# The opening of a hybrid retention and attention layer: first loads on two queues, rows scaled in two parts, products in another order

## The chip, the cores and the metric

The kernel runs on one core of a Trainium2 chip. The metric is the device time of one execution in microseconds, lower is better. Before the change the median of three runs is 1394.26 us (1393.91 to 1397.99).

A core has a matrix engine (TensorE, PE in the profile, with its weight loads shown as PEld), a vector engine (VectorE, DVE), a scalar engine (ScalarE, ACT), a general engine (GpSimd, POOL) and an engine that only issues transfers (SyncE, SP). SP and ACT can both issue transfers; each has a queue of its own, served by the same 16 DMA engines.

## The reference, cut to what matters

```python
h_lat = rms_norm(x, norm1_g) * (1.0 + sc1) + sh1        # x: 1024 x 1024, sc1 and sh1 from silu(c) @ w_mod
h_ctx = rms_norm(ctx, norm1_g) * (1.0 + csc1) + csh1    # ctx: 256 x 1024
p = h_lat @ w_in                                        # 1024 x 3584, split into heads:
# 4 heads of bidirectional chunkwise retention, 4 heads of differential attention
x = x + g1 * (concat(retention, attention) @ w_out)
h2 = rms_norm(x, norm2_g) * (1.0 + sc2) + sh2
x = x + g2 * conv_ffn(h2)                               # gated MLP with a depthwise convolution
return rms_norm(x, final_g)
```

All of it is in 32-bit floats. The change touches the first two lines and the first block of `w_in` (512 columns, the attention's values); the rest of the kernel stands as it was.

## The kernel before, in words

A product of two 32-bit matrices is made of three matrix products of rounded parts: each operand is split into a high part (rounded) and a low part (the rest), and `high x high`, `high x low` and `low x high` are summed in PSUM. `passes` issues these three (L131 to L133). ACT makes the high parts, DVE or POOL the low parts by a subtraction.

The opening works on the first 512 rows of `x` as four tiles of 128 rows (`xs0`; the order lists call them xs_171 to xs_174, here rows 0 to 3) and on the next 512 as `xs1`. The names are these:

- `cl` holds small vectors, `csil` is silu of the conditioning, spread into `cz`; `ident` is the identity that transposes use; `fold` is made of it.
- `mod_load(d, q)` loads half q of the modulation weights for the d-th 128 columns into a tile `wt`; `mod_part` multiplies them with `cz` into `pr` (L513); `mod_row` copies the result to `rw` (ACT); `mod_sums` turns it with `fold` into `pm` and makes the scale and shift `mcol` (DVE, L524 and L525).
- `square` (ACT, into `sq`) and `power` (DVE, then POOL) give a row's factor in `sm`; `scale` multiplies the row by it (DVE, L535).
- `modulate` transposes the d-th 128 columns of the rows into `pt` (PE, L541), applies `mcol` and writes the high part of `hT` (ACT, L544), the same in full into `tmp` (DVE, L546) and the low part of `hT` (L548), on POOL for odd d and on DVE for even d. `latents` calls it for `xs0` and `xs1`, `context` for the context rows. There are three `pt` banks and two `tmp` buffers.
- `w_load` loads `w_in` into `raw`, `w_split` splits it into `whi` (ACT, L569) and `wlo` (DVE, L571). A `raw` tile holds two of the eight steps k; the first is loaded and split in halves.
- `part_products(ts, k)` adds step k to the output tiles `ts`, two at a time. `turn_over` issues products of ones whose result is thrown away, while PE has nothing else.

The loop over k interleaves all this: products of tiles 0 and 1, some preparation, products of tiles 2 and 3, more preparation for later steps. From k = 6 on the second half of the rows is transposed and modulated, for two further output tiles. `in_order(begin)` at its end keeps every engine of PE, DVE, ACT and SP in the order in which the code was written. What is written first therefore goes first on its engine, and a queue waits for its head.

Of the kernel before, what the change touches and what calls it, by code (L numbers as in the profile page):

```python
# [17 lines left out]
P = 128  # L18
D = 1024
KD = D // P  # L20
# [52 lines left out]
def kernel(  # L73
# [80 lines left out]
    with ExitStack() as p1:  # L154
# [343 lines left out]
        with ExitStack() as p0:  # L498
# [38 lines left out]
            def modulate(tiles, d, who, hi, lo):  # L537
# [9 lines left out]
                eng = nc.gpsimd if d % 2 else nc.vector  # L547
# [10 lines left out]
            def w_load(kk, i0=0, i1=2):  # L558
                if i0 == 0:
                    raws.append(wr.tile([P, 2, 512], F32, name="raw"))  # L560
                nc.sync.dma_start(out=raws[-1][:, i0:i1], in_=w_in[6][:, 2 * kk + i0 : 2 * kk + i1, :])
# [20 lines left out]
            def part_products(ts, k):  # L582
                if k > 0:
                    for t in ts:
                        passes(part[t], lat_lhs(t, k), wget(k, 0, 512), False, k == KD - 1)
                    return
                hi, lo = wget(k, 0, 512)
                for t in ts:
                    mm(part[t], lat_lhs(t, k)[0], hi, start=True, stop=False)
                for t in ts:  # L590
                    mm(part[t], lat_lhs(t, k)[0], lo, start=False, stop=False)
                if 3 in ts:
                    latents(0, 1)
                for t in ts:
                    mm(part[t], lat_lhs(t, k)[1], hi, start=False, stop=False)
# [8 lines left out]
            for t in range(2):  # L604
                load_row(t, nc.scalar)
            mod_load(0, 1)
            nc.sync.dma_start(out=ident, in_=consts[:, K_ID : K_ID + P])
            w_load(0, 0, 1)
            for t in range(2, 4):
                load_row(t)  # L610
            for q in range(2):
                mod_load(1, q)
# [8 lines left out]
            turn_over(2)  # L621
# [20 lines left out]
            square(xs0[3], 5)  # L642
            power(5)
            for q in range(2):
                mod_load(3, q)
            for k in range(KD):
                part_products((0, 1), k)
                if k == 0:
# [3 lines left out]
                    scale(xs0[2], 4, 0, 2 * P)  # L652
                    scale(xs0[3], 5, 0, 2 * P)
# [24 lines left out]
                if k == 0:  # L678
                    for t in range(1, 4):
                        scale(xs0[t], 2 + t, 2 * P, D)  # L680
# [22 lines left out]
                if k in (0, 2, 4):  # L703
                    w_split()
# [926 lines left out]
```

## Time and profile before

| | us |
|---|---|
| median of three runs | 1394.26 (1393.91 to 1397.99) |
| the profiled execution | 1398.66 |
| its span | 1396.9 |
| PE busy | 1365.7 (98%) |
| DVE busy | 1003.0 (72%) |
| ACT busy | 729.6 (52%) |
| POOL busy | 296.9 (21%) |

The profile shows one execution. A row of the order in time gives start and length in us, the engine, the source line, the operation, the output and input tiles, their sizes and the count; the bracket at its end is how long the engine had been idle before it and whose completion ended that. A row may hold several instructions that follow each other. A row of a window gives the window, its length, then the busy time of PE, PEld, DVE, ACT and POOL with the number of instructions, PE's granted clock (1.00 is full), the busy share of the DMA engines and GB/s.

### The profile page before, as it was taken

To read this page: it belongs to the slowest core of one execution; us is meant where nothing else is said; L and a number is where in the kernel's file an instruction comes from. 1 tells how busy PE (TensorE), PEld (TensorE's weight loads), DVE (VectorE), ACT (ScalarE), POOL (GpSimd) and SP (SyncE) were. 2 spreads that over 40 slices of the span, in tenths; PEclk is the share of its full clock that TensorE was granted. 3 is DMA by queue.
4 is the path that set the end of the run, shared out by engine and by line. 5 is a ranking of instruction groups with operands and counts; after the bars stand their busy time and mean duration, and the time that the engine had idled before them with its cause. 6 is when DMAs were issued, how large, how long until landed. Compare 5 with 4: busy or idle time off the path is not lost.

```text
span 1396.9 us, 19447 instructions
## 1 busy us (share of the span) xinstructions
PE 1365.7 (98%) x7038; PEld 1146.9 (82%) x7038; DVE 1003.0 (72%) x1462; ACT 729.6 (52%) x1395; POOL 296.9 (21%) x321
## 2 busy tenths in 40 slices
PE   8999999999999899999999999999999999999997
PEld 5788888888887799998888788888888888888886
DVE  4655773424676798896347998777788777798757
ACT  4652222424575689997126645555445555454543
POOL 1310000001556133421201732233332220000001
PEclk9999999999999999999999999999999999999999
DMA  9546885465574696641421223323233225963523
GB/s 360 211 166 216 286 277 175 142 174 164 178 237 141 181 222 155 127 97 46 166 84 61 91 106 114 113 91 113 100 111 113 85 81 177 374 232 99 181 91 128
DMA packets 96807, 218.81 MB, mean 157 GB/s; under 512 B 9220, under 2 KB 31236, under 8 KB 96200
## 3 DMA queue, kind: packets, MB, share of 16 engines
q1 hardware_dynamic: 87976, 190.83, 40.0%
q0 software_dynamic: 8160, 24.91, 7.9%
q10 hardware_dynamic: 576, 1.84, 0.4%
q8 instruction: 55, 0.90, 0.3%
q14 instruction: 40, 0.33, 0.1%
HBM read 160.13 MB, written 57.41 MB: 156 GB/s over the span
## 4 chain that ended last, share of the span: by engine, by line
PE 86%; DMA 5%; DVE 4%; ACT 2%; issue 2%; POOL 1%; SPq 0%; POOLq 0%; ACTq 0%; DVEq 0%
PE chain L131 5%; PE chain L133 5%; PE chain L132 5%; PE pv L893 5%; PE c L132 5%; PE pA L861 5%; PE c L131 5%; PE c L133 5%; PE pn L131 4%; PE pn L133 4%; PE pn L132 4%; PE pl L133 3%; PE pl L131 3%; PE pl L132 3%; PE third L131 3%; PE third L133 3%
## 5 line engine op out<-in xcount | busy, mean ns | idle before, releaser
L131 PE MATMUL pl<-hT,whi 128*128 128x512 f32 x256 | 106.5, 416 | 0.0
L131 PE MATMUL chain<-T,whi 128*128 128x512 f32 x264 | 103.2, 392 | 0.7 <-ACT ua L1177 0.4
L132 PE MATMUL chain<-T,whi 128*128 128x512 f32 x264 | 102.8, 389 | 0.0
L133 PE MATMUL chain<-T,wlo 128*128 128x512 f32 x264 | 102.4, 389 | 0.0
L133 PE MATMUL pl<-hT,wlo 128*128 128x512 f32 x256 | 100.6, 393 | 0.0
L132 PE MATMUL pl<-hT,whi 128*128 128x512 f32 x256 | 100.4, 392 | 0.0
L864 DVE TENSOR_REDUCE mt<-pA 128x1 f32<-128x1280 f32 x64 | 95.3, 1490 | 3.7 <-PE pA L861 3.3
L861 PE MATMUL pA<-ks,qhl 128*128 128x512 f32 (+1 forms) x384 | 89.5, 369 | 3.0 <-ACT p L868 2.7
L133 PE MATMUL c<-whi,ghl 128*128 128x512 f32 x232 | 90.3, 389 | 0.0
L131 PE MATMUL c<-whi,ghl 128*128 128x512 f32 x232 | 90.3, 389 | 0.0
L132 PE MATMUL c<-wlo,ghl 128*128 128x512 f32 x232 | 90.3, 389 | 0.0
L868 ACT ACTIVATE p<-pA,mt 128x1280 f32<-128x1280 f32 x64 | 85.5, 1335 | 6.8 <-DVE mt L864 6.7
L1032 ACT CAST whi<-cmb 128x512 fp32r<-128x512 f32 x62 | 38.5, 622 | 81.1 <-PE chain L132 60.7
L861 PEld LDWEIGHTS pA<-ks,qhl 128*128 128x128 f32 x384 | 67.6, 189 | 15.2 <-ACT p L868 3.4
L893 PE MATMUL pv<-va,aT 128*128 128x128 f32 x640 | 76.9, 275 | 0.1
L131 PE MATMUL pn<-whi,hT 128*128 128x512 f32 x188 | 76.8, 409 | 0.0
L133 PE MATMUL pn<-whi,hT 128*128 128x512 f32 x188 | 73.8, 393 | 1.3 <-POOL hT L548 1.2
L1035 DVE TENSOR_TENSOR wlo<-cmb,whi 128x512 fp32r<-128x512 f32 x62 | 60.3, 974 | 20.3 <-ACT whi L1032 20.3
L1191 POOL TENSOR_TENSOR cmb<-wrb 128x512 f32<-128x512 f32 x19 | 27.8, 1462 | 221.1 <-DMA wrb<-w_up 132.0
L893 PEld LDWEIGHTS pv<-va,aT 128*128 128x128 f32 x640 | 74.0, 192 | 0.7 <-DVE yT L922 0.3
L132 PE MATMUL pn<-wlo,hT 128*128 128x512 f32 x188 | 73.7, 392 | 0.8 <-DVE wlo L571 0.8
L1032 ACT CAST whi<-wra 128x512 fp32r<-128x512 f32 x55 | 33.7, 622 | 72.8 <-PE third L132 42.5
(319 smaller groups left out, 3822.5 us busy)
## 6 DMA issues: line engine op xcount, KB each, us to landing
wm<-w_mod SPq DMA_DIRECT2D x32, 512.0 KB, 5.3
raw<-w_in SPq DMA_DIRECT2D x27, 512.0 KB, 4.6
wra<-w_up SPq DMA_DIRECT2D x24, 512.0 KB, 3.3
wrb<-w_up SPq DMA_DIRECT2D x22, 512.0 KB, 3.6
W<-w_down SPq DMA_DIRECT2D x44, 256.0 KB, 5.3
ad<-s SPq DMA_DIRECT2D x20, 512.0 KB, 3.5
wra<-ad SPq DMA_DIRECT2D x20, 512.0 KB, 3.7
kvs<-kvg SPq DMA_DIRECT2D x36, 256.0 KB, 3.1
```

The costliest lines, as they stand in the source:

```text
L131: mm(ps, lh, rh, start=first, stop=False, skip_group_check=more)
L132: mm(ps, lh, rl, start=False, stop=False, skip_group_check=more)
L133: mm(ps, ll, rh, start=False, stop=last, skip_group_check=more)
L861: mm(self.pa[m][:, c0:c1], self.q[:, m, i, qs], self.k[:, m, c0:c1], start=(i == 0), stop=(i == 1))
L864: nc.vector.tensor_reduce(out=self.mt[:, m : m + 1], in_=self.pa[m][:, :LK], axis=AX.X, op=ALU.min)
L868: nc.scalar.activation(self.p[m], self.pa[m][:, :LK], AF.Exp, scale=-1.0, bias=self.mt[:, m : m + 1], accum_out=self.s[:, m : m + 1])
L893: mm(self.pv, self.aT[:, c, :], self.v[:, c, :], start=(c == 0), stop=(c == NKT - 1))
L1032: cast = nc.scalar.copy(hi, src)
L1035: nc.vector.tensor_tensor(out=lo, in0=src, in1=r32(hi), op=ALU.subtract)
L1191: nc.gpsimd.tensor_tensor(out=s1, in0=b1, in1=b2, op=ALU.add)
```

## The change

The first loads are dealt to the two queues in another way. On ACT's queue stood the first half of the modulation weights and rows 0 and 1:

```order
L507 DMA wt<-w_mod 128x1024
L574 DMA xs_171<-x 128x1024
L574 DMA xs_172<-x 128x1024
L615 ACT_TABLE_LOAD
L615 ACTIVATE csil<-cl 128x16
L529 ACTIVATE sq,sm<-xs_171 128x1024
L517 COPY rw<-pr 128x256
L529 ACTIVATE sq,sm<-xs_172 128x1024
L569 COPY whi<-raw 128x512
L529 ACTIVATE sq,sm<-xs_173 128x1024
L544 ACTIVATE hT_167<-pt,mcol 128x256
```

Now it has five loads, and the square of row 1 comes ahead of the copy of `rw`:

```order
L507 DMA wt<-w_mod 128x1024
L574 DMA xs_171<-x 128x1024
L561 DMA raw<-w_in 128x512
L574 DMA xs_173<-x 128x1024
L507 DMA wt<-w_mod 128x1024
L611 ACT_TABLE_LOAD
L611 ACTIVATE csil<-cl 128x16
L529 ACTIVATE sq,sm<-xs_171 128x1024
L529 ACTIVATE sq,sm<-xs_172 128x1024
L517 COPY rw<-pr 128x256
L569 COPY whi<-raw 128x512
L529 ACTIVATE sq,sm<-xs_173 128x1024
```

The weight half, row 2 and the first half of the next modulation weights came over from SP, row 1 went there. `hT` still stands behind the square of row 2. On SP's queue stood, from the kernel's start:

```order
L98 DMA cl<-cols 128x260
L507 DMA wt<-w_mod 128x1024
L607 DMA ident<-consts 128x128
L561 DMA raw<-w_in 128x512
L574 DMA xs_173<-x 128x1024
L574 DMA xs_174<-x 128x1024
L507 DMA wt<-w_mod 128x1024 x2
```

and now:

```order
L98 DMA cl<-cols 128x260
L604 DMA ident<-consts 128x128
L574 DMA xs_172<-x 128x1024
L507 DMA wt<-w_mod 128x1024
L574 DMA xs_174<-x 128x1024
L507 DMA wt<-w_mod 128x1024
L561 DMA raw<-w_in 128x512
```

The first `wt` of this queue, second half of the first modulation weights, moved from second place to fourth, behind the identity and row 1.

On DVE the rows are scaled in two parts, the first 384 columns early and the other 640 later, and the low part of `hT` for d = 1 is made there instead of on POOL. At steps k = 0 and 1 of the loop the difference is (xs_172 to xs_174 are rows 1 to 3, hT_169 is the low part):

```order
 L571 TENSOR_TENSOR wlo<-raw,whi 128x512
 L546 TENSOR_SCALAR tmp<-pt,mcol 128x512
-L535 TENSOR_SCALAR xs_172<-xs_172,sm 128x768
-L535 TENSOR_SCALAR xs_173<-xs_173,sm 128x768
-L535 TENSOR_SCALAR xs_174<-xs_174,sm 128x768
+L548 TENSOR_TENSOR hT_169<-tmp,hT_167 128x512
 L571 TENSOR_TENSOR wlo<-raw,whi 128x1024
```

and a little further on:

```order
 L546 TENSOR_SCALAR tmp<-pt,mcol 128x512
 L548 TENSOR_TENSOR hT_169<-tmp,hT_167 128x512
+L535 TENSOR_SCALAR xs_173<-xs_173,sm 128x640
+L535 TENSOR_SCALAR xs_174<-xs_174,sm 128x640
 L524 TENSOR_SCALAR mcol<-pm,bsc,cl 128x2
```

Three scalings left the place ahead of the second `wlo`; two of 640 columns stand behind the low part of d = 2. The other two (rows 0 and 1) stand ahead of the first scaling of rows 2 and 3.

In the products of a block, both tiles now take their `high x high`, then both their `high x low`, then both their `low x high`, at every k and not only at k = 0. The splitting of the next weights at k = 4 goes ahead of the squares of the last two rows of `xs1`. Five warm-up products were added between the two halves of the first modulation and the six ahead of the first transposes taken out. No product of the result was added or removed.

```diff
-                eng = nc.gpsimd if d % 2 else nc.vector
+                eng = nc.gpsimd if d % 2 and d > 1 else nc.vector
...
             def part_products(ts, k):
-                if k > 0:
-                    for t in ts:
-                        passes(part[t], lat_lhs(t, k), wget(k, 0, 512), False, k == KD - 1)
-                    return
                 hi, lo = wget(k, 0, 512)
                 for t in ts:
-                    mm(part[t], lat_lhs(t, k)[0], hi, start=True, stop=False)
+                    mm(part[t], lat_lhs(t, k)[0], hi, start=(k == 0), stop=False)
                 for t in ts:
                     mm(part[t], lat_lhs(t, k)[0], lo, start=False, stop=False)
-                if 3 in ts:
+                if k == 0 and 3 in ts:
                     latents(0, 1)
                 for t in ts:
-                    mm(part[t], lat_lhs(t, k)[1], hi, start=False, stop=False)
+                    mm(part[t], lat_lhs(t, k)[1], hi, start=False, stop=(k == KD - 1))
...
             mod_load(0, 0, nc.scalar)
-            for t in range(2):
-                load_row(t, nc.scalar)
+            load_row(0, nc.scalar)
+            w_load(0, 0, 1, nc.scalar)
+            load_row(2, nc.scalar)
+            mod_load(1, 0, nc.scalar)
+            nc.sync.dma_start(out=ident, in_=consts[:, K_ID : K_ID + P])
+            load_row(1)
             mod_load(0, 1)
-            nc.sync.dma_start(out=ident, in_=consts[:, K_ID : K_ID + P])
-            w_load(0, 0, 1)
-            for t in range(2, 4):
-                load_row(t)
-            for q in range(2):
-                mod_load(1, q)
+            load_row(3)
+            mod_load(1, 1)
...
             mod_load(2, 1)
-            turn_over(2)
+            turn_over(7)
             mod_part(0, 1)
...
             square(xs0[0], 2)
             power(2)
-            mod_row(0)
-            mod_sums(0)
-            scale(xs0[0], 2)
-            turn_over(6)
+            scale(xs0[0], 2, 0, 3 * P)
             square(xs0[1], 3)
             power(3)
+            mod_row(0)
             w_split(0, 1, nc.scalar)
-            scale(xs0[1], 3, 0, 2 * P)
+            scale(xs0[1], 3, 0, 3 * P)
+            mod_sums(0)
             w_split(0, 1, nc.vector)
             square(xs0[2], 4)
-            power(4)
             latents(0, 0, 0, 2)
             square(xs0[3], 5)
+            power(4)
+            scale(xs0[0], 2, 3 * P, D)
             power(5)
+            scale(xs0[1], 3, 3 * P, D)
+            scale(xs0[2], 4, 0, 3 * P)
+            scale(xs0[3], 5, 0, 3 * P)
...
                 if k == 1:
                     mod_sums(2)
                     latents(0, 2)
+                    for t in (2, 3):
+                        scale(xs0[t], 2 + t, 3 * P, D)
...
+                if k in (0, 2, 4):
+                    w_split()
                 if k == 3:
                     square(xs1[0], 6)
...
                     power(9)
-                if k in (0, 2, 4):
-                    w_split()
```

More of the change, by code (lines that the diff above doesn't have):

```diff
@@ L556, in wget, with w_load @@
                 return tuple(t[:, k % 2, c0:c1] for t in sl[k // 2])
-            def w_load(kk, i0=0, i1=2):
+            def w_load(kk, i0=0, i1=2, eng=nc.sync):
                 if i0 == 0:
                     raws.append(wr.tile([P, 2, 512], F32, name="raw"))
-                nc.sync.dma_start(out=raws[-1][:, i0:i1], in_=w_in[6][:, 2 * kk + i0 : 2 * kk + i1, :])
+                eng.dma_start(out=raws[-1][:, i0:i1], in_=w_in[6][:, 2 * kk + i0 : 2 * kk + i1, :])
             def w_split(i0=0, i1=2, only=None):
@@ L651 @@
                     mod_row(1)
-                    scale(xs0[2], 4, 0, 2 * P)
-                    scale(xs0[3], 5, 0, 2 * P)
                     latents(0, 0, 2, 4)
@@ L678 @@
                 if k == 0:
-                    for t in range(1, 4):
-                        scale(xs0[t], 2 + t, 2 * P, D)
                     for q in range(2):
```

## The prediction

> **What bounds the kernel now.** I read the page's busy shares first, then the windows of the first 80 us, then the order of instructions in time there. Every edit lies in the work of `part_products` and what feeds it, and after it each engine's queue is the same but for line numbers and one load issued sooner. So the change can only move the moment from which TensorE (PE) runs without a break; what follows is carried along.
>
> ```profile
> PE 1365.7 (98%) x7038; PEld 1146.9 (82%) x7038; DVE 1003.0 (72%) x1462; ACT 729.6 (52%) x1395; POOL 296.9 (21%) x321
> 10.00:20.00 10.00, 7.86 (x56) 5.61 (x56) 5.81 (x19) 5.88 (x12) 2.27 (x4) 1.00 1.03 408
> 30.00:40.00 10.00, 10.00 (x75) 7.42 (x74) 4.74 (x9) 3.64 (x7) 1.30 (x1) 1.00 1.02 409
> 50.00:60.00 10.00, 9.81 (x57) 7.44 (x57) 9.90 (x14) 6.66 (x10) 3.82 (x3) 1.00 0.36 107
> 70.00:80.00 10.00, 10.00 (x51) 8.26 (x51) 6.51 (x16) 6.26 (x10) 4.80 (x6) 1.00 0.11 38
> ```
>
> The window rows give the busy time of PE, its weight loads, VectorE (DVE), ScalarE (ACT) and GpSimd (POOL), then PE's clock, the share of the DMA engines and GB/s. Between 10 and 20 us the DMA engines are full and PE is not; between 30 and 40 PE is full; between 50 and 60 DVE is (9.90 of 10); by 70 PE is full again. Three stages, three limits. Now the first, in order of time:
>
> ```profile
> 5.98 0.64 PE L513 MATMUL pr<-wt,cz 128*32 128x256 f32 x8 [0.57 <-DMA wt<-w_mod]
> 6.55 0.71 PE L599 MATMUL pn<-ones 128*128 128x128 f32 x4
> 8.10 0.64 PE L513 MATMUL pr<-wt,cz 128*32 128x256 f32 x8 [0.84 <-DMA wt<-w_mod]
> 9.48 0.35 ACT L517 COPY rw<-pr 128x256 f32<-128x256 f32 x1
> 9.50 0.16 DVE L625 TENSOR_TENSOR fold<-ident 128x2 f32<-128x2 f32 x1 [4.00 <-DMA ident<-consts]
> 10.63 1.58 PE L599 MATMUL pn<-ones 128*128 128x128 f32 x12
> 11.13 0.74 DVE L535 TENSOR_SCALAR xs<-xs,sm 128x1024 f32<-128x1024 f32 x1
> 11.37 0.62 ACT L569 CAST whi<-raw 128x512 fp32r<-128x512 f32 x1
> 12.82 1.06 ACT L529 ACTIVATE sq<-xs 128x1024 bf16<-128x1024 f32 x1 [0.83 <-DMA xs<-x]
> 13.88 0.55 ACT L544 ACTIVATE hT<-pt,mcol 128x256 fp32r<-128x256 f32 x1
> 15.04 0.43 DVE L548 TENSOR_TENSOR hT<-tmp,hT 128x256 fp32r<-128x256 f32 x1
> 15.58 0.35 DVE L535 TENSOR_SCALAR xs<-xs,sm 128x256 f32<-128x256 f32 x1
> 17.19 0.44 PE L541 MATMUL pt<-ident,xs 128*128 128x128 f32 x2
> ```
>
> The first products need `hT` at 13.88. It stands on ACT behind the square of row 2, which waited for that row's load until 12.82. The rest was there by then: the first modulation weights in two halves, called wt00 and wt01 here, at 5.98 and 8.10, whose products go through `rw`, `fold` and `mcol` into the same `hT`.
>
> **The change, part by part.** *Loads.* On ACT's queue now stand wt00, row 0, the first weight half, row 2 and a later wt; on SP's cl, the identity, row 1, wt01, row 3. So wt01 moves from second place on SP to fourth, behind row 1. When SP's queue reaches the end of wt01 and ACT's that of row 2, the bytes moved are cl 130, the identity 64, the weight half 256 and five of 128 x 1024 floats, 512 each: 3010 KB, the very set that had landed at 12.82 before. The identity's row shows that the queues take turns by small pieces: it landed at 9.50, 1.4 us after wt01, which was next ahead of it, though it is only 64 KB. So wt01 and row 2 finish nearly together. If SP's queue were instead a whole transfer ahead, wt01 would end with 2498 KB moved, all of these but row 2, and before that set was there at 11.37, when `whi` read the weight half. I bound wt01 by 11.37 and 12.82 and take 12.1, past the middle because of the identity's row. From there ACT does, in order: after the matmuls of wt01 (0.64) the copy `rw` (0.35), `whi` (0.62), the square (1.06), then `hT`: 2.67, at 14.77 instead of 13.88, or **+0.9** (+0.2 to +1.6). ACT's two further DMA issues fall before cl lands and cost nothing; the warm-up products (five more behind wt00, six fewer behind wt01) run while PE waits anyway. Row 3 and the wt of the next block come in other places of the same sum of bytes; they are read only from about 15 us on, when before they had landed too, and PE's `pr` of that block stands behind the later `hT`. That I cost at nothing; if the cover went, it would be the one transfer of 512 KB that row 3 is put back, 1.3 us at the 408 GB/s above.
>
> The Trainium skill, "DMA: Bandwidth & Descriptors", section "Queues, rings and completion order", says that a DMA engine drains a packet of some 9 to 17 descriptors from one queue before it turns to the other. By that rule wt01 would come whole before row 2, near the early bound, and this term would be +0.2. The identity's late landing speaks for finer turns.
>
> *Rows scaled in two parts.* Ahead of the scaling of rows 2 and 3, whose transposes stand at 17.19, DVE now also scales 640 columns of rows 0 and 1, and 384 in place of 256 of rows 2 and 3. Between 0.35 (256 columns) and 0.74 (1024) these come to 0.55 and 0.42. From the end of `hT`'s low part (15.47, or 1.59 after `hT` starts): two small powers (0.15 each), 2 x 0.55, 2 x 0.42, less some 0.09 of overlap each, is 1.8; with 0.1 to reach PE the transposes come 3.5 after `hT` instead of 3.31: **+0.2** (0 to +0.4).
>
> *Low part of d = 1 from POOL to DVE, products by parts, rows 2 and 3 later.*
>
> ```profile
> 21.49 2.68 DVE L535 TENSOR_SCALAR xs<-xs,sm 128x768 f32<-128x768 f32 x3
> 21.65 1.57 POOL L548 TENSOR_TENSOR hT<-tmp,hT 128x512 fp32r<-128x512 f32 x1 [5.31 <-DVE tmp L546]
> 21.70 1.05 ACT L569 CAST whi<-raw 128x1024 fp32r<-128x1024 f32 x1
> 23.28 0.50 PE L133 MATMUL pn<-whi,hT 128*128 128x512 f32 x1 [1.25 <-POOL hT L548]
> 24.09 1.21 DVE L571 TENSOR_TENSOR wlo<-raw,whi 128x1024 fp32r<-128x1024 f32 x1
> 25.23 0.27 DVE L524 TENSOR_SCALAR mcol<-pm,bsc,cl 128x2 f32<-128x2 f32 x1
> 25.72 0.78 ACT L544 ACTIVATE hT<-pt,mcol 128x512 fp32r<-128x512 f32 x1 [2.97 <-DVE mcol L525]
> 26.53 0.81 DVE L546 TENSOR_SCALAR tmp<-pt,mcol 128x512 f32<-128x512 f32 x1 [0.91 <-ACT hT L544]
> 27.38 0.69 DVE L548 TENSOR_TENSOR hT<-tmp,hT 128x512 fp32r<-128x512 f32 x1
> 28.65 0.59 PEld L513 LDWEIGHTS pr<-wt,cz 128*32 128x32 f32 x16 [0.17 <-issue]
> ```
>
> Regrouping changes no matmul, only puts those that need the low part last in each pair of tiles. POOL's 1.57 becomes 0.69 on DVE, so PE's wait of 1.25 goes. What is late next: with the 2.68 of scaling gone, DVE can start `wlo` when `whi` ends (22.75) and `mcol` can start at 24.0 (25.23 before). But then `hT`, `tmp`, `lo` and the two 640-column scalings of rows 2 and 3 follow: 24.45 + 0.81 + 0.81 + 0.69 + 2 x 0.5 = 27.8, and the next transposes now wait for row 3. They used to end as `pr` began, 28.65; now that is 28.05. So of some 1.6 only **-0.6** is left (-1.6 if the scalings hide, 0 if ACT is late too).
>
> *Weights split in front of squares, and d = 1 of the second half.*
>
> ```profile
> 45.42 1.41 DVE L535 TENSOR_SCALAR xs<-xs,sm 128x1024 f32<-128x1024 f32 x2
> 46.68 1.03 ACT L569 CAST whi<-raw 128x1024 fp32r<-128x1024 f32 x1
> 47.75 1.22 DVE L571 TENSOR_TENSOR wlo<-raw,whi 128x1024 fp32r<-128x1024 f32 x1 [0.78 <-ACT whi L569]
> 49.02 0.50 PE L132 MATMUL pn<-wlo,hT 128*128 128x512 f32 x1 [0.75 <-DVE wlo L571]
> 52.55 1.27 POOL L548 TENSOR_TENSOR hT<-tmp,hT 128x512 fp32r<-128x512 f32 x1 [4.52 <-DVE tmp L546]
> 53.22 1.15 DVE L548 TENSOR_TENSOR hT<-tmp,hT 128x512 fp32r<-128x512 f32 x1
> 62.17 0.80 DVE L546 TENSOR_SCALAR tmp<-pt,mcol 128x512 f32<-128x512 f32 x1
> 64.41 0.19 PEld L133 LDWEIGHTS pn<-whi,hT 128*128 128x128 f32 x1 [0.45 <-POOL hT L548]
> ```
>
> `whi` goes in front of two squares, so PE's wait of 0.75 at 49.02 goes. But DVE is busy without a break from 47.75 to 62.97, and PE waits for that chain's last low part at 64.41. DVE's idle 0.78 before `wlo` turns into an idle stretch of like length behind it: the squares end later, DVE must scale rows 4 and 5 (the first two of `xs1`) before the powers, and POOL's power stands between. I cost it at **0** (-0.75 to +0.3). One low part moved to DVE adds 0.69 there and takes POOL off it once, where a DVE row of 0.69 took 1.15 (53.22, beside POOL's): **+0.2** (0 to +0.7). The same edit for the context rows falls between 70 and 80 us, where DVE has 3.5 of 10 free and PE does not wait: 0.
>
> Sum: +0.9 + 0.2 - 0.6 + 0 + 0.2 = +0.7 us. The profiled execution took 1398.66 (span 1396.9), 4.4 above the median of the runs, 1394.26; I add the sum to the median: **1395.0**.
>
> **The rivals.** *Faster:* wt01 lands at the early bound and the wait at 49.02 is really won: 0.2 + 0.2 - 0.6 - 0.75 + 0.2 = -0.8, 1393.5. For it: SP issues row 1 at once. Against: DVE's 9.90 of 10.
>
> *Slower: PE's clock.* Six warm-up products took 1.58 at 10.63, 0.26 each, so seven from 6.55 end near 8.4; then PE has nothing until wt01 at 12.1, 3.7 us.
>
> ```profile
> 429.28:432.70 3.42, 1.53 (x11) 1.38 (x11) 2.68 (x7) 2.05 (x9) 2.66 (x4) 1.00 0.36 100
> 432.70:436.11 3.41, 3.41 (x13) 3.03 (x12) 2.32 (x6) 0.91 (x2) 1.49 (x3) 0.50 0.43 148
> 9.44:12.86 3.42, 2.13 (x17) 1.92 (x17) 1.93 (x9) 2.20 (x7) 1.11 (x2) 1.00 1.04 396
> ```
>
> A stretch of 3.4 us with PE busy 1.53 was followed by 3.41 us at half clock; one with 2.13 (the start as it is) was not. After the change the stretch from 9.44 holds wt01's 0.64 and the warm-up behind it, about 1.0. Half clock over a stretch where PE is short of time costs up to 3.41 / 2 = 1.7; the first such stretch is mostly waiting, so it decides if the slow clock lasts to about 19.7: one full price 1396.7, two 1398.4, and with wt01 at 12.82 as well (+0.7) 1399.1, the only sum here past the bound. The Trainium skill, "TensorE: Matmul & The Clock Gate", section "What's actually happening", has the half clock follow an idle window of about 3.4 us; by that rule a gap of 3.7 us would seldom cover a whole window and this rival would nearly vanish. The row at 429.28 shows that a busy share of 45% was enough.
>
> **How the numbers follow.** A measurement of this kernel tells about 0.3% (4.2 us) from no change; the three runs shown lie 4.1 apart. Forecast 0.5 (1394.2 to 1395.7 by wt01's bounds), faster rival 0.25, clock 0.2, something unseen 0.05. No sum reaches -4.2, so faster gets 0.04; slower 0.12, for the clock's far end and the runs' own spread; same 0.84. The range goes from below the faster rival, 1393.0, to the clock's two windows, 1398.4.
>
> **What would show it.** After: the second `pr` group near 12.1, `hT` near 14.8, no wait for POOL near 23, the transposes near 28 waiting for DVE's scaling, no wait for `wlo` near 49, the last wait for POOL's low part near 65, and behind it all shifted alike. I am wrong if wt01 lands before 11.4, if the clock shows 0.5 past 16 us, or if PE's break-free stretch begins more than 2 us from 64.4.

## The result, and the profile after

The changed kernel takes 1399.35 us (median of eight runs, 1397.30 to 1401.32), the kernel before 1394.81 beside it (1393.84 to 1397.99). The ratio is 1.0027, with an interval of 1.0017 to 1.0038: slower by 2.4 to 5.3 us, just under the 0.3% that I had named as the least one can tell, but the interval does not hold 1, and the time is outside my range. The profiled execution took 1399.35 itself, span 1397.6. The page's busy times hardly moved:

```profile
PE 1366.7 (98%) x7036; PEld 1147.3 (82%) x7036; DVE 998.4 (71%) x1466; ACT 730.0 (52%) x1395; POOL 295.1 (21%) x318
```

Three windows of ten microseconds, beside those of before:

```profile
10.00:20.00 10.00, 6.84 (x32) 4.36 (x36) 4.44 (x13) 3.94 (x9) 1.99 (x3) 0.60 1.02 417
30.00:40.00 10.00, 9.69 (x72) 6.86 (x71) 5.36 (x12) 3.25 (x5) 1.29 (x1) 1.00 1.01 387
50.00:60.00 10.00, 8.90 (x50) 6.52 (x48) 9.26 (x16) 6.30 (x11) 2.66 (x3) 1.00 0.84 311
```

In the first row PE did 32 matmul instructions where it had done 56, and its granted clock was 0.60. Stretch by stretch, in the steps in which the clock changes:

```profile
5.19:8.60 3.41, 2.57 (x24) 1.79 (x22) 0.90 (x6) 1.32 (x4) 0.00 (x0) 1.00 1.02 392
8.60:12.02 3.42, 0.00 (x0) 0.00 (x0) 1.15 (x4) 1.22 (x3) 1.11 (x2) 1.00 1.02 419
12.02:15.43 3.41, 2.92 (x17) 2.11 (x18) 0.00 (x1) 1.77 (x4) 0.00 (x0) 0.50 1.03 418
15.43:18.84 3.41, 2.75 (x7) 1.90 (x7) 3.19 (x10) 1.77 (x5) 1.14 (x2) 0.50 1.02 419
18.84:22.26 3.42, 3.42 (x22) 1.29 (x21) 0.68 (x2) 0.61 (x2) 0.29 (x1) 0.50 0.57 214
22.26:25.67 3.41, 3.41 (x30) 2.16 (x30) 2.44 (x6) 1.61 (x3) 0.00 (x0) 1.00 0.80 256
```

One stretch in which PE did nothing, then three at half clock. The order in time of that part shows why PE stood still and what came late (SPq and ACTq are the issuing of a transfer by SP and ACT):

```profile
1.66 0.42 SPq L574 DMA_DIRECT2D xs<-x  x1
5.61 0.33 SPq L507 DMA_DIRECT2D wt<-w_mod  x1
6.64 0.16 DVE L621 TENSOR_TENSOR fold<-ident 128x2 f32<-128x2 f32 x1 [0.83 <-DMA ident<-consts]
9.25 1.06 ACT L529 ACTIVATE sq<-xs 128x1024 bf16<-128x1024 f32 x1 [0.58 <-DMA xs<-x]
12.51 1.08 PE L513 MATMUL pr<-wt,cz 128*32 128x256 f32 x8 [4.25 <-DMA wt<-w_mod]
13.52 1.22 PE L595 MATMUL pn<-ones 128*128 128x128 f32 x4
13.66 0.37 ACT L517 COPY rw<-pr 128x256 f32<-128x256 f32 x1 [3.26 <-PE pr L513]
14.54 0.85 PE L523 MATMUL pm<-fold,rw 128*128 128x2 f32 x4
15.96 0.56 ACT L544 ACTIVATE hT<-pt,mcol 128x256 fp32r<-128x256 f32 x1 [0.36 <-PE pt L541]
```

Row 1 and the sums stood so before:

```profile
10.07 1.06 ACT L529 ACTIVATE sq<-xs 128x1024 bf16<-128x1024 f32 x1 [0.24 <-DMA xs<-x]
10.20 0.58 PE L523 MATMUL pm<-fold,rw 128*128 128x2 f32 x4 [0.81 <-DVE sm L113]
```

The identity and row 1 are there earlier than before (9.50 and 10.07 there), wt01 comes last, at 12.51. Its matmuls take 1.08 instead of 0.64, the two warm-up products behind it 1.22 instead of 0.71, the sums 0.85 instead of 0.58, and `hT` starts at 15.96 (13.88 before).

wt01 was also issued late. In both profiles the two queues together issue eight loads by 3.9 us, five on SP and three on ACT before, three and five now. The ninth, which is row 3 before and wt01 now, is issued only at 5.86 and 5.61, after SP has waited 2.5 and 3.5 us for the landing of a `wt`.

Further on:

```profile
31.67 0.79 PE L541 MATMUL pt<-ident,xs 128*128 128x128 f32 x2 [0.18 <-DVE xs L535]
32.39 1.07 PE L513 MATMUL pr<-wt,cz 128*32 128x256 f32 x16
49.22 1.23 DVE L571 TENSOR_TENSOR wlo<-raw,whi 128x1024 fp32r<-128x1024 f32 x1
60.39 0.66 PE L541 MATMUL pt<-ident,xs 128*128 128x128 f32 x4 [0.79 <-DVE tmp L546]
68.48 0.19 PEld L133 LDWEIGHTS pn<-whi,hT 128*128 128x128 f32 x1 [0.34 <-POOL hT L548]
```

The `pr` group that began at 28.65 begins at 32.39, the wait for `wlo` is gone, and the last wait for POOL's low part stands at 68.48 instead of 64.41: the opening is 4.07 us later. From the start of `hT` to that last wait it was 50.53 before and is 52.52 now. So 2.08 of the 4.07 lie ahead of `hT` and 1.99 behind it.

### The profile page after: what moved, and what is told of

It reads as the page before. It is cut to its first block, busy times and chain, and to the rows that moved or that the text cites. A ratio compares the mean times of both kernels' runs of the same rounds, so it can differ in the third digit from the quotient of the medians.

```text
span 1397.6 us, 19438 instructions
## 1 busy us (share of the span) xinstructions
PE 1366.7 (98%) x7036; PEld 1147.3 (82%) x7036; DVE 998.4 (71%) x1466; ACT 730.0 (52%) x1395; POOL 295.1 (21%) x318
## 4 chain that ended last, share of the span: by engine, by line
PE 86%; DMA 4%; DVE 4%; issue 2%; ACT 2%; POOL 1%; SPq 0%; POOLq 0%; ACTq 0%; DVEq 0%
PE chain L131 5%; PE chain L133 5%; PE chain L132 5%; PE pv L890 5%; PE pA L858 5%; PE c L132 4%; PE c L133 4%; PE c L131 4%; PE pn L133 3%; PE pn L131 3%; PE pn L132 3%; PE pl L133 3%; PE pl L131 3%; PE pl L132 3%; PE third L131 3%; PE third L133 3%
## 5 line engine op out<-in xcount | busy, mean ns | idle before, releaser
L1032 DVE TENSOR_TENSOR wlo<-cmb,whi 128x512 fp32r<-128x512 f32 x62 | 55.1, 890 | 19.6 <-ACT whi L1029 19.5
L131 PE MATMUL third<-yT,whi 128*128 128x512 f32 x168 | 65.5, 390 | 0.0
L132 PE MATMUL third<-yT,whi 128*128 128x512 f32 x168 | 65.4, 389 | 0.0
L133 PE MATMUL third<-yT,wlo 128*128 128x512 f32 x168 | 65.4, 389 | 0.0
```

The costliest lines, as they stand in the source:

```text
L131: mm(ps, lh, rh, start=first, stop=False, skip_group_check=more)
L132: mm(ps, lh, rl, start=False, stop=False, skip_group_check=more)
L133: mm(ps, ll, rh, start=False, stop=last, skip_group_check=more)
L1032: nc.vector.tensor_tensor(out=lo, in0=src, in1=r32(hi), op=ALU.subtract)
```

## The experiments

My theory after the result: PE's half clock, brought about by the empty stretch in front of wt01, is the larger part of the loss; the late wt01 is the rest; the edits to DVE's and PE's order are worth next to nothing. The rivals: the late loads alone are the cause, or the removal of six warm-up products, or one of the edits that I had priced at nothing.

**Four kernels first: the clock kept, the loads put back, the clock lost without the change, one edit alone.** `k1_warm` is the changed kernel with more of the thrown-away products:

```diff
-            turn_over(7)
+            turn_over(24)
...
             mod_sums(0)
+            turn_over(6)
```

> The changed kernel with 24 warm-up products instead of 7 in front of the second half of the first modulation, and six more behind its sums, so that PE works through the wait; loads and all else as changed. Theory (PE's clock): no stretch at half clock after 6 us; hT about 2.7 us after wt01 lands, so 15.2 with wt01 at 12.5; PE's last wait for POOL's low part, 64.41 before and 68.48 after the change, comes at 65.5 to 66; time 1.0 to 1.5 us above before. Rival (the late load itself costs it all): clock full, but the last wait stays at 67.5 to 68.5 and the time 3.5 to 4.5 above before.

`k2_oldloads` is the changed kernel with the loads of before, in their order, and PE kept busy in the same way:

```diff
-            load_row(0, nc.scalar)
...
+            for t in range(2):
+                load_row(t, nc.scalar)
...
-            turn_over(7)
+            turn_over(2)
             mod_part(0, 1)
             w_load(1)
-            turn_over(2)
+            turn_over(10)
...
             mod_sums(0)
+            turn_over(4)
```

> The changed kernel with the loads dealt as before, and the warm-up products placed so that PE is never idle for long (2 before the second half of the first modulation, 10 behind it, 4 behind its sums); the other edits as changed. Theory: wt01 at 8.1, hT at 13.9 as before, full clock; what is left of the change is +0.2 (scalings in two parts), -0.6 (low part on DVE, rows 2 and 3 later), 0 (split in front of squares) and +0.2 to +0.4 (second half): last wait for POOL at 64.0 to 64.6, time within 0.5 us of before. Rival (the DVE edits cost by themselves): last wait past 65.5, time 1.5 us or more above before.

`k3_cold` is the kernel before without its six warm-up products behind the first sums:

```diff
-            turn_over(6)
```

> The kernel before without its six warm-up products behind the first modulation's sums, nothing else changed: no load moves, only PE idles longer between 9 and 14 us. Theory (PE's clock, by PE's busy time in a stretch of 3.4 us): from 9.44 to 12.86 PE is then busy some 0.6 to 0.9 us, below the 1.53 that was followed by half clock, so half clock from about 12.9 for one to three stretches, the last wait for POOL 1 to 3.5 us after 64.41 and the time as much above before. Rival (a whole idle stretch is needed): full clock throughout, last wait at 64.4, time as before.

`k4_split` is the kernel before with one edit of the change, the weights split in front of the squares:

```diff
+                if k in (0, 2, 4):
+                    w_split()
                 if k == 3:
...
-                if k in (0, 2, 4):
-                    w_split()
```

> The kernel before with only the splitting of the weights at k = 4 moved in front of the squares. Theory (DVE bounds the stretch from 47.75 to 62.97): PE's wait for wlo at 49.02 is gone, but the last wait for POOL stays at 64.2 to 64.7, time as before within 0.3 us. Rival (the wait is won): last wait at 63.6 to 63.7, time 0.75 us below.

Measured: `k1_warm` 1396.30 us, ratio 1.0000 (0.9990 to 1.0010); `k2_oldloads` 1394.54, 0.9994 (0.9982 to 1.0005); `k3_cold` 1399.95, 1.0024 (1.0009 to 1.0040); `k4_split` 1395.03, 0.9997 (0.9986 to 1.0008); the kernel before beside them 1395.93. With the clock kept the changed kernel is as fast as the one before. And the kernel before, with nothing but six products of ones taken out, becomes as slow as the changed one. The stretches of `k3_cold`:

```profile
7.37:10.79 3.42, 2.12 (x18) 1.29 (x17) 0.93 (x7) 2.58 (x6) 0.56 (x1) 1.00 1.04 406
10.79:14.20 3.41, 1.37 (x3) 0.79 (x4) 2.30 (x7) 2.64 (x5) 1.10 (x2) 0.50 1.00 387
14.20:17.62 3.42, 3.42 (x18) 1.92 (x21) 1.32 (x5) 0.57 (x2) 0.61 (x1) 0.50 1.04 421
```

Half clock came as expected, but not for the reason that I had given: the stretch in front of it held 2.12 us of work and not 0.6 to 0.9, about as much as the 2.13 that kept the clock in the profile of before. The last wait came 0.89 later than before, just short of the 1 to 3.5 that I had expected. What in such a stretch sets the half clock off is not shown.

In `k1_warm` the clock is at 1.00 through the opening, yet `hT` starts no earlier:

```profile
12.92 0.64 PE L513 MATMUL pr<-wt,cz 128*32 128x256 f32 x8 [0.60 <-DMA wt<-w_mod]
14.52 1.58 PE L595 MATMUL pn<-ones 128*128 128x128 f32 x12
15.94 0.38 PE L541 MATMUL pt<-ident,xs 128*128 128x128 f32 x2
16.36 0.56 ACT L544 ACTIVATE hT<-pt,mcol 128x256 fp32r<-128x256 f32 x1 [0.80 <-PE pt L541]
66.88 0.19 PEld L133 LDWEIGHTS pn<-whi,hT 128*128 128x128 f32 x1 [0.34 <-POOL hT L548]
```

The six products that I put back stand ahead of the transposes and delay them by nearly what they take; ACT waits 0.80 for that. I had expected `hT` at 15.2, the last wait at 65.5 to 66 and a time 1.0 to 1.5 us above before; the first two came later, and the time was that of before. What the full clock wins lies behind `hT`: from there to the last wait it is 50.52, as before (50.53), and not 52.52.

`k2_oldloads` and `k4_split` answer for the other edits. The changed order with the old loads:

```profile
27.48 1.07 PE L513 MATMUL pr<-wt,cz 128*32 128x256 f32 x16
55.66 0.66 PE L541 MATMUL pt<-ident,xs 128*128 128x128 f32 x4 [0.79 <-DVE tmp L546]
63.75 0.19 PEld L133 LDWEIGHTS pn<-whi,hT 128*128 128x128 f32 x1 [0.36 <-POOL hT L548]
```

and the split alone:

```profile
49.72 0.97 PE L541 MATMUL pt<-ident,xs 128*128 128x128 f32 x5 [0.50 <-DVE xs L535]
63.76 0.19 PEld L133 LDWEIGHTS pn<-whi,hT 128*128 128x128 f32 x1 [0.43 <-POOL hT L548]
```

`hT` starts at 13.05 and 13.20 there, and at 12.94 to 13.31 in the other runs with the old loads. The loads of the profile of before had come later: row 2 was read at 12.82 there, and at 11.89 to 12.26 in `k2_oldloads`, `k3_cold`, `k4_split` and `m1_front6`, which load in the same order. So the last wait of `k4_split`, nearly the rival's 63.6 to 63.7, decides nothing by itself; the times from `hT` on do. In the first, that `pr` group comes 14.43 after `hT` (14.77 before), and from it to the last wait it is 36.27 (35.76 before): a third of a microsecond won and half of one lost. In the second, the wait for `wlo` is gone and a wait for DVE's scaling is there in its place; from `hT` to the last wait it is 50.56, so the split alone wins nothing.

**Four more: which part of the opening decides, and what the clock goes by.** `n1_swap` exchanges two transfers of the changed kernel:

```diff
             nc.sync.dma_start(out=ident, in_=consts[:, K_ID : K_ID + P])
-            load_row(1)
             mod_load(0, 1)
+            load_row(1)
             load_row(3)
```

> The changed kernel with row 1 and the second half of the first modulation weights (wt01) in exchanged places on SP; nothing else. wt01 then has 1280 KB less ahead of it (row 1, the weight half and part of row 2), some 3 us at 408 GB/s, and its products stand near 9.5 in place of 12.51, row 1's square near 10.5 in place of 9.25. Theory (the loss is PE's half clock, and six warm-up products fewer behind wt01 are enough for it): half clock still comes, a stretch or two later than at 12.02, hT near 14, 1397.5 to 1399.5. Rival (the late wt01 and the empty stretch of 4.25 us in front of it are the cause): no half clock in the first 30 us, 1395 to 1396.

Measured: 1398.15, ratio 1.0013 (0.9999 to 1.0026). The theory's numbers held for the time, but `hT` stood at 15.54, not near 14, and the reason was not in my expectation:

```profile
9.15 0.64 PE L513 MATMUL pr<-wt,cz 128*32 128x256 f32 x8 [0.93 <-DMA wt<-w_mod]
12.50 1.06 ACT L529 ACTIVATE sq<-xs 128x1024 bf16<-128x1024 f32 x1 [3.90 <-DMA xs<-x]
13.96 1.02 PE L523 MATMUL pm<-fold,rw 128*128 128x2 f32 x4 [3.53 <-ACT rw L517]
15.54 0.56 ACT L544 ACTIVATE hT<-pt,mcol 128x256 fp32r<-128x256 f32 x1
```

wt01 came 3.4 us earlier and row 1 came 3.2 later, to the very place where wt01 had been. Whichever of the two is put last lands at 12.5, and `hT` needs both. Exchanging these two mends nothing: the one put last is again the ninth load, issued at 5.48 here. And ACT's queue is ahead of SP's: in the changed kernel's profile it had moved 2.31 MB when wt01 landed, nearly all of its five loads (2.36), the next block's wt among them, and SP's queue 1.48 MB. Whether the late issue or this share sets the 12.5 was not tried. PE's empty stretch was moved and not removed: it is now 3.53 us long in front of the sums. So the rival, which needed it gone, was not put to the test. Half clock came here as well, from 12.88 to 19.71.

`n2_six` puts back only the six products, and leaves the empty stretch:

```diff
             mod_sums(0)
+            turn_over(6)
```

> The changed kernel with the six warm-up products put back behind the sums of the first block; the empty stretch of 4.25 us in front of wt01 stays. Theory (the empty stretch triggers the half clock, and how long it lasts is set by how busy PE is behind it): half clock from about 12, for one or two stretches in place of three, 1397 to 1398.5. Rival (the six products alone decide): no half clock in the first 30 us, 1395.5 to 1396.5. Third (once slow, six products more change nothing): three stretches again, 1399.4.

Measured: 1398.90, ratio 1.0023 (1.0010 to 1.0035).

```profile
10.70:14.12 3.42, 1.52 (x16) 1.07 (x16) 0.42 (x1) 0.82 (x3) 0.26 (x1) 1.00 1.03 420
14.12:17.53 3.41, 3.41 (x16) 3.08 (x16) 1.00 (x3) 1.12 (x3) 0.00 (x0) 0.50 1.03 417
```

One stretch at half clock instead of three, and yet hardly a gain: the six products themselves now run at half clock, 2.91 us, ahead of the transposes, and `hT` starts at 17.64, 1.68 later than in the changed kernel. The rival, that the six products alone decide, falls; that the empty stretch triggers the slow clock stands. The time is just above the 1397 to 1398.5 that I had given for a shorter slow stretch; I had left out that the filler stands in front of `hT`, which the rows show, though not that this is all of it.

`n3_front` was an attempt to beat both kernels: `k2_oldloads`, with `hT` no longer behind row 2's square:

```diff
-            square(xs0[2], 4)
             latents(0, 0, 0, 2)
+            square(xs0[2], 4)
```

> The kernel with the changed products, scaling, low part and split but the loads of before and PE kept warm (k2_oldloads), with the square of row 2 put behind the first two tiles of the first block, so that hT no longer waits for row 2's load. hT near 12.5 in place of 13.05, last wait for POOL's low part near 63.2, 1394.0 if the opening is carried to the end. Rival: the square of row 2 is now late for DVE's powers and scalings, the transposes of rows 2 and 3 wait, and nothing is won: 1394.5 to 1395.5.

Measured: 1395.52, ratio 0.9993 (0.9978 to 1.0009). `hT` started at 12.94 (it now waits 1.33 for its transposes, behind the filler), the last wait stood at 64.28. The rival was right: nothing is won.

`n4_narrow` asks what the clock goes by. It is `k1_warm` with fillers that use a quarter of PE's columns for the same time:

```diff
-                    mm(part[3][:, :P], ones, ones, start=True, stop=True)
+                    mm(part[3][:32, :P], ones[:, :32], ones, start=True, stop=True)
```

> The changed kernel with the same number of warm-up products as k1_warm (which kept full clock, 1396.3), but each uses 32 of the 128 columns of PE instead of all; they take PE's time as before. If the clock goes by PE's busy time: full clock, 1396.3, mean clock 0.998. Rival, by which the slow stretches with PE busy 2.75 and 2.92 of 3.41 us did not end the half clock because products of 32 or 2 columns count for less: half clock again in the first 30 us, mean clock 0.996 or less, 1398 to 1400.

Measured: 1397.75 beside 1395.86 of the kernel before, ratio 1.0003 (0.9990 to 1.0016), mean clock 0.997 to 0.999 in its executions. (The ratios are those on record; the ratio of the two medians differs from them by up to 0.0011, here and in `m2_fill`.)

```profile
9.46:12.87 3.41, 2.44 (x25) 2.15 (x27) 0.79 (x3) 0.78 (x2) 0.55 (x1) 1.00 1.03 420
12.87:16.28 3.41, 3.29 (x30) 2.39 (x22) 1.00 (x3) 1.95 (x5) 0.00 (x0) 1.00 1.03 414
```

Narrow products kept the clock as wide ones do; the rival falls. That speaks against narrow products as the reason why the slow clock lasted through stretches with PE busy 2.92 and 2.75 of 3.41 us; whether they can end a slow stretch was not tried.

**A last four: the odd result, the filler alone, the changed kernel again.** `k3_cold` had lost 4 us though its last wait stood at 65.30, only 1.5 later than in `k4_split`. `m1_front6` moves the six products to the very start instead of taking them out:

```diff
-            turn_over(9)
+            turn_over(15)
...
-            turn_over(6)
```

> The kernel before, with the six warm-up products not left out, as in k3_cold, but moved from behind the sums of the first block to the very start, where PE is busy anyway: the same instructions in number, the same empty stretch behind the sums. k3_cold lost 4 us although its last wait for POOL's low part stood only 1.5 later. Theory (PE's half clock in the opening): half clock in the first 20 us again, 1398 to 1400. Rival (not the clock, but the six instructions fewer, which shift what comes later in the program): clock 0.998 or not, the time is that of before, 1395 to 1396.

Measured: 1397.48 beside 1396.41 of the kernel before, ratio 1.0012 (1.0000 to 1.0024), mean clock 0.993 to 0.997 in all ten executions. Half clock came again, and with it the last wait stood at 67.43:

```profile
9.67:13.08 3.41, 1.23 (x6) 0.80 (x6) 2.04 (x8) 2.52 (x4) 1.11 (x2) 1.00 1.02 398
13.08:16.49 3.41, 2.58 (x6) 1.82 (x6) 2.13 (x7) 1.82 (x5) 1.16 (x2) 0.50 1.02 411
16.49:19.91 3.42, 3.42 (x23) 1.60 (x22) 0.00 (x0) 0.92 (x3) 0.00 (x0) 0.50 1.03 422
19.91:23.32 3.41, 3.41 (x12) 2.71 (x11) 1.89 (x5) 0.83 (x3) 0.00 (x0) 0.50 0.86 326
```

The loss, 1.7 us by the ratio, is less than the 3.3 of `k3_cold`, and the time stays below the 1398 to 1400 I had expected, with an interval that touches 1. That the same number of instructions with the same gap behind the sums loses its clock is shown; that all of `k3_cold`'s loss comes from that is not.

`m2_fill` fills the empty stretch of the changed kernel and puts nothing in front of `hT`:

```diff
-            turn_over(7)
+            turn_over(24)
```

> The changed kernel with the empty stretch ahead of wt01 filled (24 warm-up products in place of 7) and nothing put back behind the sums of the first block. Theory (what is lost is hT's later start and the half clock): if the full stretch keeps the clock, hT 2.7 behind wt01's landing at 12.5 to 12.9, so 15.2 to 15.6, last wait near 66, 1395.5 to 1397. If the sums' own gap is enough for half clock, as in the kernel before without its six products: one or two slow stretches, 1398 to 1399.5.

Measured: 1396.35, ratio 0.9989 (0.9976 to 1.0001).

```profile
11.83:15.24 3.41, 2.15 (x20) 1.32 (x18) 0.60 (x3) 1.67 (x3) 0.00 (x0) 1.00 1.03 418
15.24:18.66 3.42, 2.65 (x6) 1.82 (x6) 2.89 (x9) 1.76 (x5) 1.43 (x2) 0.50 1.03 418
```

```profile
12.86 0.64 PE L513 MATMUL pr<-wt,cz 128*32 128x256 f32 x8 [0.90 <-DMA wt<-w_mod]
15.40 0.56 ACT L544 ACTIVATE hT<-pt,mcol 128x256 fp32r<-128x256 f32 x1
```

`hT` started at 15.40, 2.54 after wt01's products at 12.86: at full clock my chain from wt01 to `hT` is right. But the sums' own gap still leaves a stretch with 2.15, and in the profiled execution half clock followed, to 25.48, with the last wait at 69.52. The mean clocks of its ten executions run from 0.995 to 0.999; the four slowest are all at 0.997 or below, the three at 0.998 and above took 1393.91 to 1394.39, some 2 us below the median of the other seven (1396.40).

`m4_fill2` closes that gap too, with four products behind the transposes, where PE had waited 1.14 us for `hT`:

```diff
             latents(0, 0, 0, 2)
+            turn_over(4)
```

> m2_fill with four more warm-up products between the transposes of the first block and its first products, where PE waited 1.14 us for hT in m2_fill, so that they delay nothing. m2_fill had half clock in about half of its executions by their mean clock (0.995 to 0.999). Theory (the half clock is what still cost there): mean clock 0.998 or more in nearly all, hT 15.4, last wait near 66, 1395 to 1396, and with the loads' own delay left a time like k1_warm's or 0.5 to 1 below. Rival (half clock comes as before, since the products count for less than their time): 1396.4 and mean clocks spread from 0.995 to 0.999 as in m2_fill.

Measured: 1397.43, ratio 1.0008 (0.9999 to 1.0018). The opening is what I wanted, with the clock at 1.00 throughout, `hT` at 14.78 and the last wait at 65.24. The time is not: seven of the eleven executions have a mean clock of 0.997 or less, and the profiled one, at 0.997, has a slow stretch in the middle of the kernel:

```profile
444.87:448.28 3.41, 0.91 (x7) 0.45 (x5) 3.38 (x7) 1.20 (x3) 2.23 (x3) 1.00 0.54 205
448.28:451.69 3.41, 3.41 (x10) 2.73 (x9) 1.39 (x3) 0.89 (x2) 3.41 (x7) 0.50 0.80 175
```

`m3_after2` is the changed kernel again, on the chip of `m1_front6` and `m2_fill`.

> The changed kernel as it is, on the chip of these runs, for a second profile. Theory: half clock from 11 to 14 us on for two to three stretches in every execution (mean clock 0.993 to 0.996), hT 15.5 to 16.5, 1399.4. Rival (the first profile was an odd one): hT near 15, mean clock 0.997 or more in half of the executions, 1396.

Measured: 1400.13, ratio 1.0022 (1.0010 to 1.0034), mean clock 0.993 to 0.996 in all ten executions; `hT` at 15.94, three stretches at half clock from 12.06, the last wait at 68.47. In `hT` and the last wait it repeats the first profile to 0.02 us, and it has one more slow stretch in the middle:

```profile
8.65:12.06 3.41, 0.00 (x0) 0.00 (x0) 1.10 (x4) 1.15 (x2) 1.11 (x2) 1.00 1.02 419
370.47:373.88 3.41, 1.38 (x9) 0.95 (x8) 0.94 (x3) 2.59 (x11) 1.01 (x1) 1.00 0.87 288
373.88:377.29 3.41, 3.41 (x14) 3.03 (x13) 2.47 (x5) 0.00 (x0) 1.24 (x2) 0.50 0.15 55
```

All of it in one table, sorted by the clock of the opening in the profiled execution (last wait: the last wait of PE for POOL's low part; in the two columns before the ratio, us from the start):

| kernel | loads | half clock in the opening | `hT` | last wait | ratio to before (interval) |
|---|---|---|---|---|---|
| n3_front | old | none | 12.94 | 64.28 | 0.9993 (0.9978 to 1.0009) |
| k2_oldloads | old | none | 13.05 | 63.75 | 0.9994 (0.9982 to 1.0005) |
| k4_split | old | none | 13.20 | 63.76 | 0.9997 (0.9986 to 1.0008) |
| k1_warm | new | none | 16.36 | 66.88 | 1.0000 (0.9990 to 1.0010) |
| n4_narrow | new | none | 16.27 | 66.77 | 1.0003 (0.9990 to 1.0016) |
| m4_fill2 | new | none | 14.78 | 65.24 | 1.0008 (0.9999 to 1.0018) |
| m2_fill | new | 15.24 to 25.48, not in all executions | 15.40 | 69.52 | 0.9989 (0.9976 to 1.0001) |
| m1_front6 | old | 13.08 to 23.32 | 13.31 | 67.43 | 1.0012 (1.0000 to 1.0024) |
| n1_swap | new, two exchanged | 12.88 to 19.71 | 15.54 | 67.23 | 1.0013 (0.9999 to 1.0026) |
| n2_six | new | 14.12 to 17.53 | 17.64 | 68.15 | 1.0023 (1.0010 to 1.0035) |
| k3_cold | old | 10.79 to 17.62 | 13.18 | 65.30 | 1.0024 (1.0009 to 1.0040) |
| the change | new | 12.02 to 22.26 | 15.96 | 68.48 | 1.0027 (1.0017 to 1.0038) |
| the change again | new | 12.06 to 22.30 | 15.94 | 68.47 | 1.0022 (1.0010 to 1.0034) |

With the clock kept in the profiled opening, the ratios are 0.9993 to 1.0008; with half clock there, 1.0012 to 1.0027. `m2_fill`, whose mean clocks run from 0.995 to 0.999, stands apart from both. By the means of these groups the half clock costs 0.21%, some 2.9 us (1.0020 against 0.9999); it is 0.18% among the kernels with the new loads and 0.23% among those with the old. The new loads, at full clock, cost 0.09%, some 1.3 us (1.0004 against 0.9995), with intervals that overlap, and 0.15% by the ratios of the medians. None of the kernels beats both of the two with certainty; `k2_oldloads`, `n3_front` and `m2_fill` are faster than the changed kernel and cannot be told from the one before.

The stretches are known for the profiled executions only. For the others there is a mean clock, which does not say where the slow stretches lie. It also counts the end of the span: in every profile the last 3.9 to 7.8 us run at half clock, with PE done, and that alone takes 0.0014 to 0.0028 off the mean. So 0.997 can come without another slow stretch. In the kernel before some executions stand as low as 0.993 to 0.995 too; whether those lose their clock in the opening, where its stretches of 2.13 and 2.12 are near the border, is not known.

## Why the prediction was wrong, point by point

I had forecast 1395.0 and a range to 1398.4; the kernel takes 1399.35. **The step that failed is the price of nothing for the emptier opening:** the warm-up products "run while PE waits anyway", and so PE's half clock stood outside the sum, as the rival "Slower: PE's clock", to which I gave a chance of 0.2 and at most two full prices. In place of nothing the profile shows 0.90 us for it ahead of `hT` and 1.99 behind. Only the rival's far end, with wt01 at its late bound as well, came to 1399.1 and so past the range. Half clock is there in both profiles of the changed kernel, and the mean clock is 0.993 to 0.996 in all of its 18 executions. My own rows said so: I had counted about 1.0 us of work in the stretch from 9.44, beside a row in which 1.53 was followed by half clock and one in which 2.13 was not. The count belonged below the first of these, so the slow clock was the forecast and not a rival. In the run that stretch lay from 8.60 and held nothing; the stretches begin at another time in each profile (9.44 in that of before, 8.60 and 8.65 in those of the change). I was also wrong on how long it would last: I took one or two stretches, to about 19.7, and it was three, to 22.26. Two of my three signs of being wrong came: the clock at 0.50 past 16 us, and the last wait more than 2 us from 64.4.

- *wt01's landing.* I bounded it by 11.37 and 12.82 and took 12.1. It was read at 12.51; in the kernels that keep this order of loads the row stands between 12.23 and 12.92. In the changed kernel the bounds held and my value was 0.4 early; 12.86 and 12.92 lie just past the late one. That it came so near is partly luck, for the sum of bytes behind it did not hold. I had counted 3010 KB (3.08 MB) at the landing of wt01, with row 2 finishing beside it; the two queues had moved 3.79 MB, and ACT's was nearly through the next wt, which stands behind row 2 there. In the first 6 us ACT's queue moved 0.91 MB in 240 packets and SP's only 0.21 MB in 285: the two were nearer level in packets than in bytes, and the vectors and the identity at the head of SP's queue go in small ones (1040 and 512 bytes to a row). The Trainium skill, "DMA: Bandwidth & Descriptors", section "Queues, rings and completion order", whose rule of whole packets would, as I applied it, have put wt01 near the early bound, is not borne out in that by these seven profiles: none is near 11.4.
- *2.67 from wt01 to `hT`.* Right at full clock: 2.54 in `m2_fill` and 2.55 in `m4_fill2`. In the changed kernel it was 3.45. So of the 2.08 us ahead of `hT`, 12.51 + 2.55 - 13.88 = 1.18 is the late load, where I had +0.9, and 0.90 is the half clock. Against the `hT` of 13.2 or so in the other profiles with the old loads, the late load is nearer 1.9, past my +1.6.
- *The warm-up products "run while PE waits anyway".* This was the costing at nothing that hid the fault. In `k3_cold` the kernel loses 3.3 us without six of them, and with them its clock; `m1_front6`, as many instructions and the clock lost all the same, loses 1.7. In `n2_six` the six take 2.91 us at half clock in front of `hT`, which starts 1.68 later than in the changed kernel.
- *Rows in two parts, +0.2, and the low part and order of products, -0.6.* Together -0.4; `k2_oldloads` gives -0.34 up to that `pr` group: the `hT` of rows 2 and 3 comes 4.06 us behind the first, 3.78 before, so +0.28, and the rest is -0.62. The wait for DVE's scaling stands where I had put it (31.67 in the changed kernel). Right.
- *Split in front of the squares, 0.* `k4_split`: 50.56 from `hT` to the last wait against 50.53. The wait for `wlo` goes and comes back as a wait for `xs`. Right, and the faster rival, which needed this gain, falls.
- *One more low part on DVE, +0.2 (0 to 0.7).* With the split it is +0.5 in `k2_oldloads` (36.27 against 35.76); the place seems to be the wait of 0.79 for `tmp`. Inside its bounds.
- *Behind the opening all shifted alike.* For the kernel as it is, the sum by the rows is 1.18 + 0.90 + 1.99 = 4.07 us (4.7 against the 63.76 of `k4_split`), against 2.4 to 5.3 measured. As a rule it does not hold. `k1_warm` and `n4_narrow` open 3.0 to 3.1 later than `k2_oldloads` and `k4_split` and lose 0.4 to 1.3 us against them; `k3_cold` opens 1.5 later and loses 3.8.

What stays open is this last point. From the last wait to the end of the span it is 1326.4 to 1329.3 us in the nine profiles with no slow stretch between the opening and the end, and 1329.8 to 1333.6 in the five with one (the profile of before is one of these, 1332.5, with its slow stretch at 432.70). So a single profile does not carry a difference of 2 us, and the slow stretches in the middle, if they come in as many executions as profiles, blur the medians by as much. Whether the loss of the opening makes such a stretch more or less likely, or is in part made up where PE waits for transfers between 330 and 480 us, was not settled.

## What to carry to other kernels

Before a change takes filler products out of a thin opening, or moves a load behind which PE waits, add up PE's busy time in every stretch of 3.4 us that would result, wherever it may begin; if one may fall to 2.2 us or below, put the slow clock into the forecast (here 2.15 and less was followed by it in openings, though not every time), with what it does to the chain behind it, and not among the rivals. Filler belongs where PE waits for another engine, not in front of work that the critical chain needs. When first loads are dealt to two queues, look at when each is issued and at what the other queue moves meanwhile: here two more loads on ACT came into the first eight, wt01 became the ninth, and the last transfer that `hT` needs by its data landed at 12.51 (wt01), where it had been 10.07 (row 1).

## What the runs showed of the hardware that I had not expected

- **The clock falls long before PE is idle.** Away from the opening a stretch of 3.41 us with PE busy 0.91, 1.38, 1.53, 1.55 or 1.57 was followed by half clock every time, while the emptiest that was not had 1.63 (`n3_front`, from 351.67). In the opening the border is not sharp: 2.12 (`k3_cold`) and 2.15 (`m2_fill`) were followed by it, 2.12 and 2.13 (before) and 2.44 (`n4_narrow`) were not, nor was one of 1.49 in `n2_six`, the first for which its profile gives a clock. The Trainium skill, "TensorE: Matmul & The Clock Gate", section "What's actually happening", has the throttled state follow an idle window of some 3.4 us; the stretch from 8.60 agrees with that, the others show that work in nearly half a window (1.57 of 3.41) is not enough either.
- **In these profiles it came back only after a full stretch, and not always after the first.** At half clock, stretches with PE busy 1.37 to 2.98 of 3.41 us did not end it, in six profiles. A full one ended it in `k3_cold`, `n1_swap`, `n2_six` and in both profiles of the changed kernel; in `m1_front6` and `m2_fill` it took two. The five slow stretches in mid-kernel were all full, and none lasted longer than one.
- **Products on a quarter of the columns keep the clock up as well as those on all** (`n4_narrow`, clock 1.00 through the opening).
- **The time of the kernel before splits by its clock.** In the four sets of runs beside the experiments its executions with a mean clock of 0.998 and above have medians of 1394.8 to 1396.0, those below 1396.8 to 1398.1. A few per mille between two medians can be such stray stretches. The mean clock of an execution helps to tell, but the slow end of the span is in it too.
- **The ninth load of the opening waited for a landing.** In the profiles of before and after it was issued at 5.86 and 5.61, after 2.5 and 3.5 us of waiting, with five and three of the first eight on SP's queue. What sets this was not tried.
